# A second buffer for RWKV's chunk decay, and the decayed operands made ahead of the substitution

## The chip, the cores and the metric

The kernel runs on one core of a Trainium2 chip. The metric is the device time of one launch in microseconds; the lower, the better. The engines are named TensorE (PE, with its weight loads as PEld), VectorE (DVE), ScalarE (ACT), GpSimd (POOL) and SyncE (SP), which here issues most DMA transfers.

## What is computed

A decoder trunk of two layers on 512 tokens of width 1024, in f32. Each layer has a SwiGLU half step, a mixer of three head groups (forgetting attention "FoX", RWKV-7 time mixing, block-sparse attention "MoBA"), cross attention to 256 memory tokens, and a second SwiGLU half step. The change touches the RWKV part alone. What matters of the reference:

```python
def step(state, inp):
    r_t, w_t, k_t, v_t, kk_t, a_t = inp
    sa = jnp.einsum('bhij,bhj->bhi', state, -kk_t)
    state = (state * w_t[:, :, None, :] + sa[..., None] * (kk_t * a_t)[:, :, None, :]
             + v_t[..., None] * k_t[:, :, None, :])
    return state, jnp.einsum('bhij,bhj->bhi', state, r_t)
...
_, ys = lax.scan(step, state0, xs)
y = ys.transpose(1, 0, 2, 3)
mean = jnp.mean(y, axis=-1, keepdims=True)
var = jnp.mean(jnp.square(y - mean), axis=-1, keepdims=True)
y = ((y - mean) * lax.rsqrt(var + RWKV_GN_EPS)).reshape(B, S, W) * ln_w + ln_b
```

There are eight RWKV heads of 64. The recurrence over 512 tokens is done in eight chunks of 64 tokens.

## The kernel before

TensorE multiplies each f32 projection as three products of split operands (`three`, lines 153 to 155; the same in `ztok`, lines 952 to 954), and so most of the time goes to projections whose weights stream from HBM through a ring of three buffers.

In the mixer, RWKV heads go in four pairs (hp = 0 to 3), one head on each half of the 128 partitions. Each pair passes six stages, and `ORDER` (lines 37 and 38) names them in the order in which they are written: s (`rwkv_scaled`), g (`rwkv_gram`), r (`rwkv_rows`), i (`rwkv_inverse`), t (`rwkv_transitions`), y (`rwkv_states`), mixed with projections (R, K, V, p, fq, fk, fv, mq, mk, mv) and with attention blocks (f01, f10, ...). A scheduler turns this into one fixed order of instructions for each engine: it takes what is ready by priority (`PRI` gives leads to stages), against a timeline of its own, and a tile whose buffer is still being read holds back the instruction that would write it. On the chip each engine then works through its own queue in order. So a new buffer or an edit in one stage can move instructions of other stages.

The names in the stages:
- `Dt` (line 663) is the decay from the chunk's start to each token, and `DC` (line 668) is its last column, the decay over the whole chunk, copied out by VectorE (line 669). `DC` has one buffer; `Dt` has one too.
- `ER` holds the decayed kk and r, `B` holds b and u divided by the decay (lines 683 and 702). The Gram stage multiplies `B` with `ER` (line 722) and evicts masked products into `G` and `BN` (line 726).
- The substitution (lines 741 to 745) inverts 16x16 blocks of `G` by 30 small instructions on GpSimd. Its input `A` goes from `G` through DRAM (`scA`) by DMA, its results `Pf` and `Tf` return through DRAM as well. The inverse stage reads them (line 814 first).
- In the rows stage line 789 multiplies `B` in place with `DC` on GpSimd (`ENG["B2"]` is "g"), TensorE transposes the product (line 793), ScalarE evicts it into `BN`.
- The states stage is a serial chain over the chunks: a matmul of `AR` with the state (line 907), then two VectorE updates (line 911) that multiply the old state with `DC`. After it come a group norm (lines 920 to 925) and transposes (line 932).

Helper lines: 283 is every `tt` (so the substitution, B2 and others show as L283), 278 and 276 are copies on VectorE and ScalarE, 1023 scales a softmax row, 1026 transposes it.

## Time and profile before

| | us |
|---|---|
| runs, median of 3 | 2562.94 (2560.49 to 2565.93) |
| profiled execution, its own time | 2553.76 |
| its span, first to last instruction | 2552.1 |
| TensorE busy | 2470.5 (97%) |
| VectorE busy | 1339.3 (52%) |
| ScalarE busy | 860.2 (34%) |
| GpSimd busy | 490.0 (19%) |

A share of busy time is a mean over stages with different limits. The mixer of layer 0 lies between about 400 and 760 us of the span, that of layer 1 between about 1660 and 2020. Where TensorE waits there is read from the waits, and what else ran at that moment from the instructions in order of time; the granted clock of TensorE is given for each stretch as a share of full speed.

### The profile page before, as it was taken

The numbers are of one execution on the slowest core, as the hardware profiler recorded it, in microseconds if no ns is written. First come the engines' busy times: TensorE is split into PE (matmuls) and PEld (weight loads), VectorE is DVE, ScalarE is ACT, GpSimd is POOL, SyncE is SP. The second block draws the span as 40 slices with busy tenths as digits, with TensorE's granted clock in tenths as the row PEclk, the third lists the DMA queues.
The fourth block names the chain that finished last, engine by engine and source line by source line (L and its number), as shares of the span: only waits on it lengthen the run. The fifth ranks groups of instructions, "written<-read, shape, count | busy, mean of one in ns | idle before, by whom it ended". The sixth has DMA issues, their size and how long they took to land.

```text
span 2552.1 us, 35229 instructions
## 1 busy us (share of the span) xinstructions
PE 2470.5 (97%) x13976; PEld 2019.5 (79%) x13976; DVE 1339.3 (52%) x2503; ACT 860.2 (34%) x1401; POOL 490.0 (19%) x612
## 2 busy tenths in 40 slices
PE   8999999899889899999999999999999898999999
PEld 7888887688767788888888888877877677888887
DVE  6444345666765564343444444465776666544443
ACT  4222233233353352232332222332334543422221
POOL 4212030222210122020221111202322110311211
PEclk9999999899989999999999999999989999999999
DMA  4333343221212133333333333422211220333332
GB/s 151 99 91 96 102 121 91 52 74 36 68 55 79 50 94 99 93 97 99 91 100 99 97 98 93 129 76 67 63 46 49 69 85 28 114 99 100 99 94 80
DMA packets 434881, 218.42 MB, mean 86 GB/s; under 512 B 63856, under 2 KB 428828, under 8 KB 434716
## 3 DMA queue, kind: packets, MB, share of 16 engines
q1 hardware_dynamic: 431948, 212.36, 29.3%
q10 hardware_dynamic: 2448, 2.76, 0.3%
q8 instruction: 110, 1.80, 0.3%
q0 software_dynamic: 320, 1.05, 0.1%
q14 instruction: 55, 0.45, 0.1%
HBM read 205.64 MB, written 10.49 MB: 85 GB/s over the span
## 4 chain that ended last, share of the span: by engine, by line
PE 88%; DVE 4%; POOL 3%; DMA 2%; ACT 1%; issue 1%; SPq 1%; POOLq 0%; DVEq 0%; ACTq 0%
PE acc L153 23%; PE acc L154 23%; PE acc L155 23%; PE acc L952 1%; PE po L1055 1%; PE acc L954 1%; PE acc L953 1%; PE sp L1043 1%; PE sp L153 1%; PE sp L154 1%; PE sp L155 1%; POOL P L283 1%; PE ty L722 1%; POOL T L283 1%; PE ts L862 1%
## 5 line engine op out<-in xcount | busy, mean ns | idle before, releaser
L146 ACT ACTIVATE whi<-wraw 128x1024 fp32r<-128x1024 f32 (+3 forms) x386 | 389.7, 1012 | 1147.2 <-PE acc L154 1040.6
L153 PE MATMUL acc<-xh,whi 128*128 128x512 f32 x1776 | 697.2, 394 | 7.3 <-DVE p L500 5.1
L155 PE MATMUL acc<-xh,wlo 128*128 128x512 f32 x1776 | 695.5, 392 | 0.0
L154 PE MATMUL acc<-xl,whi 128*128 128x512 f32 x1776 | 695.4, 392 | 0.0
L147 DVE TENSOR_TENSOR wlo<-wraw,whi 128x1024 fp32r<-128x1024 f32 (+3 forms) x386 | 533.7, 1384 | 128.2 <-ACT whi L146 125.7
L153 PEld LDWEIGHTS acc<-xh,whi 128*128 128x128 f32 x1776 | 334.9, 189 | 83.7 <-DVE p L500 7.4
L155 PEld LDWEIGHTS acc<-xh,wlo 128*128 128x128 f32 x1776 | 335.0, 189 | 72.1 <-DVE wlo L147 1.0
L154 PEld LDWEIGHTS acc<-xl,whi 128*128 128x128 f32 x1776 | 335.3, 189 | 69.8
L343 POOL TENSOR_TENSOR up<-up,g 128x512 f32<-128x512 f32 x88 | 123.1, 1399 | 994.8 <-ACT whi L146 868.0
L154 PE MATMUL acc<-tl,whi 128*128 128x512 f32 x704 | 273.9, 389 | 0.0
L153 PE MATMUL acc<-th,whi 128*128 128x512 f32 x704 | 273.5, 389 | 0.0
L155 PE MATMUL acc<-th,wlo 128*128 128x512 f32 x704 | 273.4, 389 | 0.0
L342 DVE TENSOR_TENSOR up<-acc,rsb 128x512 f32<-128x512 f32 x88 | 60.8, 691 | 276.0 <-PE acc L155 276.0
L296 DVE SCALAR_TENSOR_TENSOR x<-acc,x 128x512 f32<-128x512 f32 x96 | 65.9, 690 | 265.6 <-PE acc L155 265.6
L339 DVE TENSOR_TENSOR g<-acc,rsb 128x512 f32<-128x512 f32 x88 | 60.8, 691 | 199.5 <-PE acc L155 196.5
L154 PEld LDWEIGHTS acc<-tl,whi 128*128 128x128 f32 x704 | 132.2, 188 | 27.4
L153 PEld LDWEIGHTS acc<-th,whi 128*128 128x128 f32 x704 | 132.2, 188 | 27.4
L155 PEld LDWEIGHTS acc<-th,wlo 128*128 128x128 f32 x704 | 132.2, 188 | 27.3
L241 POOL TENSOR_TENSOR sqacc<-sqacc,sq 128x512 f32<-128x512 f32 x48 | 77.1, 1607 | 360.8 <-ACT sq L240 360.5
L347 POOL TENSOR_TENSOR tl<-up,th 128x512 fp32r<-128x512 f32 x88 | 128.1, 1456 | 63.9 <-ACT th L346 63.9
L346 ACT ACTIVATE th<-up 128x512 fp32r<-128x512 f32 x88 | 55.7, 633 | 124.9 <-POOL up L343 124.9
L952 PE MATMUL acc<-whi,xh 128*128 128x256 f32 x256 | 77.2, 302 | 0.3 <-DVE p L500 0.3
(354 smaller groups left out, 3091.2 us busy)
## 6 DMA issues: line engine op xcount, KB each, us to landing
wraw<-in_ffn_w_in_dram SPq DMA_DIRECT2D x176, 512.0 KB
wraw<-in_ffn_w_out_dram SPq DMA_DIRECT2D x64, 512.0 KB
wraw<-in_mix_w_in_dram SPq DMA_DIRECT2D x52, 512.0 KB
wraw<-in_ffn_w_out_dram SPq DMA_DIRECT2D x32, 384.0 KB
wraw<-in_xattn_w_kv_dram SPq DMA_DIRECT2D x16, 512.0 KB
wraw<-in_mix_w_out_dram SPq DMA_DIRECT2D x16, 384.0 KB
scx<-x SPq DMA_DIRECT2D x16, 256.0 KB
x<-scx SPq DMA_DIRECT2D x16, 256.0 KB
```

What stands on the lines that cost most here:

```text
L146: nc.scalar.activation(hv, v, AF.Copy)
L147: nc.vector.tensor_sub(lv, v, f32(hv))
L153: mm(ps, lh, rh, start=start, stop=False)
L154: mm(ps, lh, rl, start=False, stop=False)
L155: mm(ps, ll, rh, start=False, stop=stop)
L241: (nc.vector if m == KC - 1 else nc.gpsimd).tensor_tensor(self.sqacc, self.sqacc, sq, op=ALU.add)
L296: self.nc.vector.scalar_tensor_tensor(xm, ps, coef, xm, op0=ALU.mult, op1=ALU.add)
L339: nc.vector.tensor_tensor(g, pss[0], rsb, op=ALU.mult)
L342: nc.vector.tensor_tensor(up, pss[1], rsb, op=ALU.mult)
L343: nc.gpsimd.tensor_tensor(up, up, g, op=ALU.mult)
L347: nc.gpsimd.tensor_tensor(tl, up, f32(th), op=ALU.subtract)
L952: mm(o, a, wh[:, kk, :], start=k == 0, stop=False)
```

## The change

`DC` gets two buffers, and the product of `B` with `DC` (line 789) moves from the rows stage to the Gram stage, behind the masked evictions and ahead of the DMA transfers and the substitution. Engine and shape stay.

```diff
-RW = {"e": 2, "tk1": 2, "tk2": 2, "zr": 2, "zv": 2, "ER": 2, "zk": 2, "BN": 2}
+RW = {"e": 2, "tk1": 2, "tk2": 2, "zr": 2, "zv": 2, "ER": 2, "zk": 2, "BN": 2, "DC": 2}
...
                     nc.vector.tensor_tensor(dst, pg[h][:, :, i], self.gmask[:, i:i + 1, :].to_broadcast([P, 4, 64]), op=ALU.mult)
             yield
 
+        B2 = B.rearrange("p q (i a) b -> p (q i) (a b)", i=2)
+        self.tt("B2", B2, B2, st["DC"].to_broadcast([P, 8, P]), ALU.mult)
+
         scA, scP, scT = (x[hp % 2] for x in (self.scA, self.scP, self.scT))
...
         self.cp("x", KX[:, :, 1, :], px)
         yield
-
         B2 = B.rearrange("p q (i a) b -> p (q i) (a b)", i=2)
-        self.tt("B2", B2, B2, st["DC"].to_broadcast([P, 8, P]), ALU.mult)
         for q in range(2):
```

What this does to the order is shown at three places. Line numbers of the change are up to three higher than before behind line 728.

GpSimd, layer 1, third head pair, before: `T` and `P` are the substitution's two tiles, and `B<-B,DC` is the moved product.

```order
L283 TENSOR_TENSOR T_14815<-A_14809,P_14814 64x2x14
L283 TENSOR_TENSOR P_14814<-P_14814,T_14815 64x2x14
L283 TENSOR_TENSOR B<-B,DC 128x1024
L664 MEMSET Dt 128x8
L283 TENSOR_TENSOR T_14815<-A_14809,P_14814 64x15
L283 TENSOR_TENSOR P_14814<-P_14814,T_14815 64x15
L747 COPY I_14848<-P_14814 64x256
```

GpSimd, the same place in the change:

```order
L283 TENSOR_TENSOR B<-a,Di 128x4x128
L664 MEMSET Dt 128x8
L283 TENSOR_TENSOR pT<-p 128x1024
L901 MEMSET tk_15095 128x512
L283 TENSOR_TENSOR B<-B,DC 128x1024
L283 TENSOR_TENSOR u<-zk,u 128x512
L283 TENSOR_TENSOR T_14816<-A_14810,P_14815 64x15
L283 TENSOR_TENSOR P_14815<-P_14815,T_14816 64x15
```

The product moved from inside the substitution to ahead of its first instruction. It stood inside in the last pair of both layers too; in the second pair of both layers and the third of layer 0 it stood behind the substitution; in the first pair of both it stood ahead already. In the change it stands ahead in all eight. In layer 0's third pair `pT<-p` (the squares of the MoBA keys) and `u<-zk,u`, which stood ahead of the substitution, now stand inside it.

VectorE, layer 0, second head pair, before: the start of its state updates (`tk_4945`, L911), among the softmax instructions of attention.

```order
L278 COPY mk<-sp 128x512
L911 SCALAR_TENSOR_TENSOR tk_4945<-tk_4945,DC,ts 64x64 x2
L1020 TENSOR_REDUCE mx<-sp 128x1 x2
L911 SCALAR_TENSOR_TENSOR tk_4945<-tk_4945,DC,ts 64x64 x2
L1022 RECIPROCAL sm<-sm 128x1
L1023 TENSOR_SCALAR p<-p,sm 128x256
```

VectorE, the same updates in the change (L912), from behind the second of them. Lines 994 and 1001 are the norm and gain of the MoBA keys, and their RoPE (L1006 to L1009) follows.

```order
L270 SCALAR_TENSOR_TENSOR hr<-rt,ry 128x16
L994 TENSOR_TENSOR p<-p,hr 128x1024
L684 SCALAR_TENSOR_TENSOR zr<-zr,params_80,u 128x512
L912 SCALAR_TENSOR_TENSOR tk_4945<-tk_4945,DC,ts 64x64 x2
L1001 TENSOR_TENSOR p<-p,gm 128x1024
```

The updates moved from among attention's instructions to among the keys' norm and RoPE. The copies of `DC` moved as well: the second pair's stood behind the first pair's last update, and now stands in the pair's own scaling stage, ahead of all of them.

TensorE, end of layer 1's mixer, before: the last state matmul of the last head pair (L907), its gate (L928, L929), and the transposes of the normed states (L932). `mhl` is the memory, whose key projection the triples of L153 to L155 are.

```order
L154 MATMUL acc<-mhl,whi 128x256
L155 MATMUL acc<-mhl,wlo 128x256
L907 MATMUL ts<-tk_16200,AR 128x128
L928 MATMUL ts<-gs_13077,g_16197 128x512
L929 MATMUL ts<-gs_13116,g_16197 128x512
L932 MATMUL ts<-ident,tk_16241 128x128 x4
L1026 MATMUL pt<-ident,p 128x128 x4
```

TensorE, the same place in the change, from the gate on (now L929, L930):

```order
L929 MATMUL ts<-gs_13077,g_16197 128x512
L930 MATMUL ts<-gs_13116,g_16197 128x512
L153 MATMUL acc<-mhl,whi 128x256
L154 MATMUL acc<-mhl,whi 128x256
L155 MATMUL acc<-mhl,wlo 128x256
```

With these three, 21 matmuls of that projection stand between the gate and the transposes (now L933), where none stood; the state chain of the last pair moved ahead of them. In layer 0 this place reads as before.

## Rows read from the trace of the kernel before

**Rows 1.** The page: busy time, share of the span and instructions of each engine; and the chain of work that ended last, by engine.

```profile
PE 2470.5 (97%) x13976; PEld 2019.5 (79%) x13976; DVE 1339.3 (52%) x2503; ACT 860.2 (34%) x1401; POOL 490.0 (19%) x612
...
PE 88%; DVE 4%; POOL 3%; DMA 2%; ACT 1%; issue 1%; SPq 1%; POOLq 0%; DVEq 0%; ACTq 0%
```

**Rows 2.** Busy time in stretches of 10 us of the two mixer stages: the stretch, its length, then busy us (and instructions) of PE, PEld, DVE, ACT and POOL, the granted clock, the share of the DMA engines and GB/s. The first three are of layer 0, the others of layer 1.

```profile
610.00:620.00 10.00, 9.36 (x66) 7.31 (x66) 6.89 (x24) 2.82 (x11) 7.61 (x27) 1.00 0.02 3
...
690.00:700.00 10.00, 6.32 (x33) 4.27 (x32) 5.35 (x12) 3.56 (x8) 4.55 (x13) 0.84 0.14 14
700.00:710.00 10.00, 9.14 (x138) 6.85 (x136) 3.83 (x10) 3.42 (x9) 0.00 (x0) 0.82 0.24 54
...
1820.00:1830.00 10.00, 8.65 (x78) 6.52 (x78) 9.06 (x31) 4.73 (x10) 2.55 (x6) 1.00 0.53 115
...
1870.00:1880.00 10.00, 7.24 (x52) 5.50 (x51) 7.88 (x22) 5.14 (x15) 7.16 (x20) 1.00 0.00 0
1880.00:1890.00 10.00, 10.00 (x58) 6.18 (x57) 4.22 (x14) 2.60 (x6) 1.24 (x4) 0.56 0.34 60
```

**Rows 3.** What TensorE waited for: the waiting engine, tile and line, the releaser, then us in total, times, the longest. The first two rows are of layer 0 (480 to 760 us), the last two of layer 1 (1800 to 2020 us).

```profile
PE pt L1026 <- DVE p L1023: 3.3, 2, 2.7
...
PE ty L793 <- POOL B L283: 0.9, 2, 0.5
...
PE pt L1026 <- DVE p L1023: 2.3, 1, 2.3
...
PE ty L793 <- POOL zt L523: 1.4, 1, 1.4
```

**Rows 4.** Layer 1, third head pair, all engines in order of time: start us, us, engine, line, operation, tiles, and the idle time before it with its releaser.

```profile
1875.56 0.29 DVE L1023 TENSOR_SCALAR p<-p,sm 128x128 f32<-128x128 f32 x1
...
1877.01 0.17 DVE L669 COPY DC<-Dt 128x8 f32<-128x8 f32 x1
...
1877.29 2.06 DVE L1023 TENSOR_SCALAR p<-p,sm 128x128 f32<-128x128 f32 x1
1877.33 1.89 POOL L283 TENSOR_TENSOR B<-B,DC 128x1024 f32<-128x1024 f32 x1 [1.56 <-DVE sm L1022]
...
1879.50 0.30 PE L1026 MATMUL pt<-ident,p 128*128 128x128 f32 x1 [2.29 <-DVE p L1023]
```

**Rows 5.** Layer 0, fourth head pair, the same view.

```profile
686.51 1.89 POOL L283 TENSOR_TENSOR B<-B,DC 128x1024 f32<-128x1024 f32 x1
...
686.75 1.68 DVE L269 SCALAR_TENSOR_TENSOR rt<-rt,ry 128x8 f32<-128x8 f32 x1
...
687.81 0.23 PE L1049 MATMUL sp<-maskb,identb 128*128 128x128 bf16 x1
...
689.38 1.02 PE L1043 MATMUL sp<-fox,qz 128*128 128x512 f32 x2
```

**Rows 6.** Groups of GpSimd's instructions, each shape apart: count, busy us, mean ns of one, and the idle time before them in all with what ended it.

```profile
L283 POOL TENSOR_TENSOR B<-B,DC 128x1024 f32<-128x1024 f32 x8 | 15.2, 1903 | 7.1 <-PE ty L722 4.5 <-DVE sm L1022 1.6 <-PE sp L1049 1.0
...
L283 POOL TENSOR_TENSOR u<-zk,u 128x512 f32<-128x512 f32 x8 | 10.3, 1291 | 43.7 <-DVE u L674 22.6 <-DVE rt L269 15.5 <-DVE ry L270 5.6
...
L283 POOL TENSOR_TENSOR pT<-p 128x1024 f32<-128x1024 f32 x4 | 9.0, 2256 | 46.5 <-ACT p L971 46.5
```

**Rows 7.** Layer 0 in order of time: the first pair's Gram evictions on VectorE with the product beside them and the mask product behind; and the first instruction of the second pair's substitution.

```profile
481.13 0.43 DVE L726 TENSOR_TENSOR G<-ty,gmask 128x256 f32<-128x256 f32 x1 [1.91 <-PE ty L722]
481.28 1.90 POOL L283 TENSOR_TENSOR B<-B,DC 128x1024 f32<-128x1024 f32 x1 [2.85 <-PE ty L722]
481.47 0.41 DVE L726 TENSOR_TENSOR BN<-ty,gmask 128x256 f32<-128x256 f32 x1
...
482.54 1.89 DVE L283 TENSOR_TENSOR tk<-G,lmask 64x512 f32<-64x512 f32 x2
...
549.38 0.22 POOL L283 TENSOR_TENSOR T<-A,P 64x15 f32<-64x15 f32 x1 [14.68 <-DMA A<-scA]
```

**Rows 8.** End of layer 1's mixer, TensorE in order of time: two matmuls of the memory's projection, one behind the other, the second half of the gate, and the transposes of the normed states.

```profile
1992.55 0.28 PE L155 MATMUL acc<-mhl,wlo 128*128 128x256 f32 x1
1992.67 0.28 PE L153 MATMUL acc<-mhl,whi 128*128 128x256 f32 x1
...
2000.98 1.12 PE L929 MATMUL ts<-gs,g 32*128 32x512 f32 x2
2006.08 1.08 PE L932 MATMUL ts<-ident,tk 128*128 128x128 f32 x4 [3.98 <-DVE tk L925]
```

**Rows 9.** Layer 0's mixer: groups of VectorE's instructions (count, busy us, mean ns of one), and one state step of the second head pair on TensorE in order of time.

```profile
L911 DVE SCALAR_TENSOR_TENSOR tk<-tk,DC,ts 64x64 f32<-64x64 f32 x48 | 13.3, 277 | 4.4 <-PE ts L907 3.4
...
L283 DVE TENSOR_TENSOR tk<-G,lmask 64x512 f32<-64x512 f32 x8 | 6.0, 748 | 0.1
...
L684 DVE SCALAR_TENSOR_TENSOR zr<-zr,params,u 128x512 f32<-128x512 f32 x4 | 3.0, 746 | 1.6 <-POOL u L283 1.5
...
L993 DVE TENSOR_TENSOR p<-p,hr 128x1024 f32<-128x1024 f32 x2 | 2.4, 1224 | 0.0
L1000 DVE TENSOR_TENSOR p<-p,gm 128x1024 f32<-128x1024 f32 x2 | 2.4, 1224 | 0.0
...
617.07 0.49 PE L907 MATMUL ts<-tk,AR 128*128 128x128 f32 x2
617.39 0.56 PE L905 MATMUL ts<-KV,BN 128*128 128x64 f32 x4
```

## Prediction

> **What bounds the kernel.** I read the page first: TensorE is busy for 2470.5 of 2552.1 us, and the chain that ended last is TensorE for 88% [rows 1]. So the kernel is bound by TensorE, and a change that adds or removes no matmul can act only on the 82 us in which TensorE stands idle and on the clock that it is granted. Next I read the busy time by stretches in the two layers' mixer stages, where the edited code runs [rows 2]: look there for stretches with little TensorE time, and for the stretch behind them in which the granted clock is below 1.00. Then I read what TensorE waited for [rows 3], and at the two worst places the instructions of all engines in order of time [rows 4, 5].
>
> In those rows the moved product, which I call B2 (B times DC, line 789, on GpSimd), appears as a releaser and as something worse. TensorE's transposes of B2 (L793) waited 0.9 us in layer 0 and 1.4 us in layer 1 [rows 3]; that last wait is booked to a tiny memset that stands right behind B2 on GpSimd. In layer 1, third head pair, B2 started at 1877.33, as soon as DC had been copied (1877.01 to 1877.18); it took 1.89 us, and for that whole time a VectorE multiply of 128x128 that had taken 0.29 us a moment earlier took 2.06. TensorE's transpose of that multiply's result waited 2.29 us [rows 4]. In the 10 us around this place TensorE was busy for 7.24 only, and in the next 10 us the granted clock was 0.56, that is near the lower of its two levels (1.2 of 2.4 GHz), while TensorE was busy throughout [rows 2]. In layer 0, fourth head pair, B2 at 686.51 held a 128x8 instruction of VectorE for 1.68 us, and TensorE, done at 688.04, got its next matmul at about 689.3 [rows 5].
>
> **The change part by part.** No instruction is added or removed: eight B2 of 1.90 us [rows 6], eight DC copies, the same transposes.
>
> *Second DC buffer.* With one buffer the copy of a head pair's DC stands on VectorE behind the state updates (L911) of the pair before it, and all that reads or overwrites what the copy reads (the next pair's Dt, then its ER product) stands behind the copy. With two buffers the copy of the second pair moves up into its own scaling stage. In the order of the change the pair after it gets its ER product ahead of, not behind, the previous pair's state updates. The buffer costs 8 floats a partition and no time.
>
> *B2 ahead of the substitution.* In six of the eight head pairs B2 moves on GpSimd from behind or inside the substitution to ahead of it; the first pair of each layer had it there already. Ahead of the substitution GpSimd waits for the round trip of G through DRAM anyway: 14.68 us in the second pair of layer 0 [rows 7]. So six times 1.90 us of GpSimd lie in a wait of that kind and cost nothing; if that cover were gone, the substitution would start 1.9 us later each time. Where B2 stood inside the substitution (the last pair of layer 0, the last two of layer 1) the inverse can start 1.9 us earlier, and another 1.6 us where B2 itself waited [rows 4].
>
> *What TensorE gets back.* The direct waits: 0.9 + 1.4 [rows 3] + 2.3 [rows 4] + 1.2 [rows 5] = 5.8 us. Bounds 2.3 (only the waits on the transposes) and 8.5 (with the 2.7 us that the next softmax step of layer 0 waited [rows 3]). I take 5.8, since each has its B2 beside it.
>
> *The clock.* 10 us at 0.56 cost 4.4 us of full speed [rows 2]. Where TensorE was idle for only 1.35 of 10 us (1820 to 1830) the clock stayed at 1.00. Without the 2.29 us wait the stretch before the drop would stand at about 0.5 idle. Bounds: 0 (it drops anyway) and 7.0 (layer 0 too: 6.32 us busy at 0.84 and 9.14 at 0.82 over 690 to 710 cost 1.0 + 1.6). I take 4.4, layer 1 alone, because in layer 0 the 2.7 us softmax wait stays.
>
> *End of layer 1's mixer.* There TensorE waited 3.98 us for the group norm of the last pair's states (L932) [rows 8]. In the order of the change the last pair's chain stands earlier, and 21 projection matmuls that stood ahead of the chain's end stand inside that wait. At 0.12 us each [rows 8] they fill 2.5 us of it. Bounds 0 (if the chain itself slips back) and 2.5. I take 2.5. In layer 0 the order there is unchanged.
>
> *What it costs in layer 0.* The order of the change puts the second pair's state updates between RoPE's instructions on VectorE, where attention stood before. Between the third and seventh of them VectorE has two 128x1024 products (2 x 1.22), L684 (0.75), four small products (estimate 0.9, from the 1.22 by width) and five pairs of updates (5 x 0.55): 6.9 us [rows 9]. TensorE has five steps of about 0.85 us (0.88 from the start of one to its end [rows 9]) and, by the order, some 1.0 us of other matmuls in that time, 5.25 in all, so it idles about 1.6 us; the stretch in which the chain lay before had 0.64 us of idle [rows 2], so 1.0 more. Since each step also hands over twice between the engines I take 1.5; bounds 0 and 6 (1.5 and a clock drop like the 4.4 of layer 1). Also, the third pair's substitution now has in its middle a square of 2.26 us and a product of 1.29 [rows 6] that stood ahead of it: its result lands up to 3.5 us later. Bounds 0 and 3.5; I take 1.0, since attention stands between.
>
> *VectorE beside B2.* In the first pair, where B2 stands in the Gram stage already, the evictions of G next to it take their usual 0.41 to 0.43 us, and the two mask products behind them took 1.89 [rows 7] where two take 1.5 by the mean [rows 9]: 0.4 us of VectorE that only the inverse, many us later, needs. So I count the moved collisions at nothing. The Trainium skill, page "SBUF — State Buffer", section "SBUF: two separate sides", says that GpSimd and VectorE share a port pair as an exclusive lock for a whole instruction, so that the loser blocks; it speaks against any move of B2 next to VectorE work with two SBUF inputs. The rows of 1.68, 1.89 and 2.06 us agree with it. By it all six moved B2 would cost VectorE at least those 0.4 us each, and if all of that were on the path the sum would be 2.4 us smaller.
>
> Sum: 5.8 + 4.4 + 2.5 - 1.5 - 1.0 = 10.2 us. The rows are of one execution of 2553.8 us (span 2552.1, so 1.7 us lie around it), for which the sum gives 2543.6. The median of the runs is 2562.9, 9.1 above that execution, so I take the 10 us off the median: **2553 us**.
>
> **The rivals.** *The gaps form again elsewhere.* The order of 300 us per layer is laid anew. In layer 0 the third pair's seven state steps (0.88 us each, 6 us in all [rows 9]) leave the attention stretch before 700 and now stand among projections, where TensorE had no gap. Attention then has less to fill its softmax waits, such as the 2.7 us one [rows 3]. Speaking for it: TensorE's work is the same, and the softmax chains that it waits for are no shorter. Against it: the waits that B2 makes are gone in any case. If the 5.8 us come back as new waits, and half of the 4.4 us of clock with them, 2.2 us are left: 2561, no change. *A queue stall, slower.* In layer 0's third pair GpSimd's in-order queue now has the square of the MoBA keys inside the substitution. It waits for ScalarE's copy of the projection; the four such squares waited 46.5 us in all, 11.6 each [rows 6]. If the keys come late, the substitution stands still behind it, its result lands 11 us late, and TensorE, whose inverse stands right behind, waits and loses clock (4.4): 2562.9 - 10.2 + 11.6 + 4.4 = 2569. It decides from a stall of some 10 us; against it speaks that the keys' projection stands ahead of the stretch in TensorE's order. *The change does nothing:* excluded, the order shows B2 moved in six of eight places.
>
> **How the numbers follow.** Forecast 0.50, gaps again 0.31, queue stall 0.19. Of the second I give 0.02 to the faster side, of the third 0.02 to no change. A difference within 0.2% (5.1 us) is no change here. Faster 0.52, same 0.31, slower 0.17. The forecast's own range goes from 2545 (8.5 + 7.0 + 2.5 and no cost) to 2557 (5.8 and the 2.5, without the clock, at the costs taken, would give 2557). The range for all is 2544 to 2568.
>
> **What would show it.** In the profile after, B2 stands ahead of the substitution's first instruction in all eight pairs; TensorE no longer waits for GpSimd at the transposes; no VectorE instruction of a softmax or a group norm takes 1.5 us or more beside B2; the granted clock of layer 1's third pair stays at 1.00; the wait for the last group norm of layer 1 is about 1.5 us where it was 3.98. I am wrong if TensorE's idle time in the mixer stages is not smaller, if the clock drops in layer 0's second pair of states, or if GpSimd stands still inside a substitution.

## The result and the profile after

| | before | change |
|---|---|---|
| median of 10 runs, us | 2557.64 (2540.47 to 2567.18) | 2582.25 (2569.5 to 2591.46) |
| ratio, 95% interval | | 1.0097 [1.0073, 1.0121] |
| profiled execution, its span, us | 2553.76, 2552.1 | 2587.9, 2586.2 |

The change is some 25 us slower, where 10 us less was forecast; the time lies above the range. (The median before, 2562.94 us of three runs in the prediction, is 2557.64 of ten.) The page after, busy time by engine and the engines of the chain that ended last (compare [rows 1]):

```profile
PE 2495.2 (96%) x13976; PEld 2036.8 (79%) x13976; DVE 1340.7 (52%) x2503; ACT 860.5 (33%) x1401; POOL 495.8 (19%) x612
...
PE 86%; DVE 5%; POOL 3%; DMA 3%; issue 2%; ACT 1%; SPq 1%; POOLq 0%; DVEq 0%; ACTq 0%
```

The same 13976 matmuls are busy 24.7 us longer, and the rest of the span grew by 9.4 us (91.0 after, 81.6 before). So of 34.1 us most is matmuls that ran slower, not TensorE standing still. The stretches of the mixers after, in the columns of [rows 2], show where (the last four are of layer 1):

```profile
600.00:610.00 10.00, 9.88 (x82) 7.91 (x79) 5.76 (x11) 5.66 (x11) 4.73 (x9) 1.00 0.45 113
610.00:620.00 10.00, 5.29 (x28) 4.21 (x28) 9.52 (x24) 0.00 (x0) 8.67 (x20) 0.75 0.00 0
620.00:630.00 10.00, 9.61 (x67) 8.30 (x66) 5.60 (x15) 4.00 (x9) 2.61 (x8) 0.57 0.31 52
...
710.00:720.00 10.00, 5.59 (x55) 4.31 (x56) 2.14 (x6) 2.35 (x7) 0.00 (x0) 0.70 0.30 60
720.00:730.00 10.00, 10.00 (x120) 7.29 (x117) 2.38 (x6) 1.82 (x5) 0.00 (x0) 0.50 0.01 2
730.00:740.00 10.00, 10.00 (x68) 6.82 (x66) 3.95 (x9) 2.85 (x9) 0.52 (x1) 0.61 0.01 2
...
1980.00:1990.00 10.00, 7.53 (x55) 4.52 (x57) 5.16 (x18) 2.40 (x6) 0.00 (x0) 0.86 0.41 77
1990.00:2000.00 10.00, 10.00 (x121) 7.32 (x118) 3.70 (x9) 3.60 (x8) 0.53 (x1) 0.50 0.01 2
...
2030.00:2040.00 10.00, 6.77 (x44) 5.05 (x42) 5.85 (x25) 3.39 (x5) 0.00 (x0) 1.00 0.16 52
2040.00:2050.00 10.00, 7.27 (x47) 6.17 (x48) 5.40 (x13) 7.06 (x20) 7.50 (x6) 0.66 0.57 184
```

Each time a stretch with little TensorE time is followed by one with a granted clock of 0.50 to 0.66: 0.50 is the lower of the two levels, what lies between is a mean of both. In the first three of these TensorE is busy for 9.6 to 10 of the 10 us, in the last for 7.27. What TensorE waited for, layer 0 (400 to 800 us) and then layer 1 (1660 to 2060):

```profile
PE pt L1027 <- DVE p L1024: 4.9, 4, 1.9
PE ts L908 <- DVE tk L912: 4.6, 4, 3.3
PE ty L815 <- DMA Tf<-scT: 4.0, 4, 3.2
...
PE ts L933 <- DVE tk L926: 3.4, 1, 3.4
PE ty L815 <- DMA Tf<-scT: 2.9, 2, 2.5
```

The same waits before (lines one lower, and the same two windows):

```profile
PE ty L814 <- DMA Tf<-scT: 2.8, 3, 1.7
PE ts L907 <- DVE tk L911: 1.8, 4, 0.9
...
PE ty L814 <- DMA Tf<-scT: 0.5, 1, 0.5
```

TensorE's waits for B2 [rows 3] are gone. Two waits that were there before have grown: those of the state steps (L908, the matmul behind the updates L912; the longest in layer 0 went from 0.9 to 3.3 us) and those of the inverse's first matmul (L815), which waits for `Tf` to return through DRAM (the longest from 1.7 to 3.2 us in layer 0 and from 0.5 to 2.5 in layer 1). I call the two places in layer 0 A and B. A, the second pair's states, all engines in order of time:

```profile
604.80 0.34 POOL L283 TENSOR_TENSOR T<-A,P 64x15 f32<-64x15 f32 x1 [7.24 <-DMA A<-scA]
...
607.28 1.89 POOL L283 TENSOR_TENSOR pT<-p 128x1024 f32<-128x1024 f32 x1
609.13 0.26 POOL L283 TENSOR_TENSOR P<-P,T 64x39 f32<-64x39 f32 x1
609.20 1.22 DVE L991 TENSOR_REDUCE hr<-pT 128x16 f32<-128x1024 f32 x1 [2.88 <-POOL pT L283]
...
614.53 1.38 DVE L269 SCALAR_TENSOR_TENSOR rt<-rt,ry 128x16 f32<-128x16 f32 x1
614.63 1.25 POOL L283 TENSOR_TENSOR u<-zk,u 128x512 f32<-128x512 f32 x1
...
616.58 0.80 PE L908 MATMUL ts<-tk,AR 128*128 128x128 f32 x2 [3.30 <-DVE tk L912]
```

VectorE's keys' norm (L991) waits for the squares, which stand inside GpSimd's substitution; behind it on VectorE stand the state updates, and TensorE waits for those. VectorE itself was busy for 9.52 of the 10 us from 610 on. L269 takes 1.38 us beside `u`, where its neighbours of that shape took 0.17 and 0.28. The Trainium skill, page "SBUF — State Buffer", section "SBUF: two separate sides", calls the port pair of the two engines a lock for a whole instruction, which the engine that starts first holds; this row agrees as to its end, 0.03 us behind that of `u`, though by the profile L269 had started 0.10 us ahead of `u`. B, the fourth pair:

```profile
682.60 1.90 POOL L283 TENSOR_TENSOR B<-B,DC 128x1024 f32<-128x1024 f32 x1 [8.48 <-PE ty L722]
...
695.57 0.22 POOL L283 TENSOR_TENSOR T<-A,P 64x15 f32<-64x15 f32 x1 [11.07 <-DMA A<-scA]
...
714.82 0.47 PE L815 MATMUL ty<-Tf,tk 64*64 64x64 f32 x2 [3.22 <-DMA Tf<-scT]
```

B2 was made 13 us ahead of the substitution and on GpSimd hid under its wait, as forecast. On VectorE it was not free:

```profile
682.66 2.05 DVE L1024 TENSOR_SCALAR p<-p,sm 128x384 f32<-128x384 f32 x1
684.64 0.41 DVE L726 TENSOR_TENSOR G<-ty,gmask 128x256 f32<-128x256 f32 x1
684.86 0.52 PE L1027 MATMUL pt<-ident,p 128*128 128x128 f32 x3 [1.02 <-DVE p L1024]
```

A softmax multiply beside B2 took 2.05 us (in layer 1's last pair 1.83, where the one ahead of B2 took 0.40). TensorE waited 1.02 us for it, and the evictions of `G`, which begin the round trip that ends with `Tf`, stood behind it.

To compare runs I cut each mixer at the first Gram matmul and at the sum of the next norm, and added up, in stretches of 5 us, idle time (length less TensorE busy) and clock loss (busy times one minus the granted clock). Length less both was 343 to 348 us in every mixer whose split is given here but those with added matmuls. "Fox gates" is the stage from L561 to layer 1's first Gram matmul, "A" and "B" are idle + clock loss in layer 0 from 120 to 190 and from 205 to 270 us behind the first Gram matmul.

| us | layer 0 (idle, clock) | A | B | fox gates, layer 1 | layer 1 (idle, clock) |
|---|---|---|---|---|---|
| before | 375.8 (21.4, 9.7) | 3.1+0.0 | 6.8+3.2 | 40.3 | 377.4 (19.5, 10.8) |
| change | 396.8 (28.4, 24.7) | 5.5+5.6 | 9.7+12.5 | 47.0 | 384.2 (21.4, 18.6) |

Layer 0's mixer is 21.0 us longer, layer 1's 6.8. The 6.7 us of the fox gates are not the change's: their order is the same in all kernels, and the stage took 39 to 43 or 45 to 47 us in kernels of every kind, before in both ways (47.0 in layer 0, 40.3 in layer 1). Two such stages can account for scatter of several us between runs, and for the profiled pair differing by 34 us where the medians differ by 25. The mixers scatter less: e1 and e2 below have the orders of the change and of before, and their four mixers (395.4 and 384.4, 375.0 and 378.1 us) lie within 1.4 us of these.

In layer 1 the change gains at one place and loses at the other. In the stretch that is called A in layer 0 its idle time and clock loss went from 4.6+6.6 to 3.9+3.3 us, 4.0 less, since the collision of [rows 4] and the drop behind it are gone; in that of B they went from 2.4+0.0 to 4.1+7.8, 9.5 more, behind the wait of 2.5 us for `Tf`.

### The profile page after: what moved, and what is told of

The parts are those of the page before. It is cut to its first block, busy times and chain, and to the rows that moved or that the text cites. A ratio compares the mean times of both kernels' runs of the same rounds, so it can differ in the third digit from the quotient of the medians.

```text
span 2586.2 us, 35235 instructions
## 1 busy us (share of the span) xinstructions
PE 2495.2 (96%) x13976; PEld 2036.8 (79%) x13976; DVE 1340.7 (52%) x2503; ACT 860.5 (33%) x1401; POOL 495.8 (19%) x612
## 4 chain that ended last, share of the span: by engine, by line
PE 86%; DVE 5%; POOL 3%; DMA 3%; issue 2%; ACT 1%; SPq 1%; POOLq 0%; DVEq 0%; ACTq 0%
PE acc L153 23%; PE acc L154 22%; PE acc L155 22%; PE po L1056 1%; PE sp L1044 1%; POOL T L283 1%; POOL P L283 1%; PE acc L953 1%; PE sp L153 1%; PE sp L154 1%; PE sp L155 1%; PE acc L954 1%; PE acc L955 1%; PE pt L1027 1%; PE ts L863 1%
## 5 line engine op out<-in xcount | busy, mean ns | idle before, releaser
L153 PE MATMUL acc<-xh,whi 128*128 128x512 f32 x1776 | 700.0, 395 | 5.8 <-DVE p L500 4.3
L155 PE MATMUL acc<-xh,wlo 128*128 128x512 f32 x1776 | 698.0, 393 | 0.0
L153 PEld LDWEIGHTS acc<-xh,whi 128*128 128x128 f32 x1776 | 336.4, 189 | 83.6 <-DVE p L500 5.6
L155 PEld LDWEIGHTS acc<-xh,wlo 128*128 128x128 f32 x1776 | 336.1, 189 | 72.5 <-DVE wlo L147 1.0
L153 PE MATMUL acc<-th,whi 128*128 128x512 f32 x704 | 273.6, 390 | 0.0
L155 PE MATMUL acc<-th,wlo 128*128 128x512 f32 x704 | 273.5, 389 | 0.0
L153 PEld LDWEIGHTS acc<-th,whi 128*128 128x128 f32 x704 | 132.2, 188 | 27.5
L155 PEld LDWEIGHTS acc<-th,wlo 128*128 128x128 f32 x704 | 132.1, 188 | 27.4
```

What stands on the lines that cost most here:

```text
L153: mm(ps, lh, rh, start=start, stop=False)
L155: mm(ps, ll, rh, start=False, stop=stop)
```

## The experiments

The experiments are numbered e1 to e18, with the number at each result. A result begins with the ratio of the medians to the kernel before, run beside it, and its 95% interval, then the median in us; what follows is of one profiled execution: the length of each layer's mixer, and A and B as idle time + clock loss. Diffs are cut to what matters. Lines that a table of waits names differ by up to nine between kernels, where text was added; the tile names are the same.

**Which half.**

```diff
-RW = {"e": 2, ..., "BN": 2}
+RW = {"e": 2, ..., "BN": 2, "DC": 2}
```

> Two buffers for DC, B2 left in the text of rwkv_rows. The order on all five engines is then, row for row, that of the changed kernel, so the line that moves B2 does nothing by itself. Theory A (the order laid anew makes the loss): ratio to the kernel before 1.007 to 1.012, as the changed kernel. Rival B (the place of B2 in the text, with what it does to GpSimd, makes the loss): the same order cannot differ, so B has to be false as far as the text goes; a ratio near 1.000 would mean that something other than the order counts (addresses, code).

Measured, e1: 1.009 [1.0064, 1.0117], 2577.17 us; layer 0 395.4 us, layer 1 384.4. The order of all engines is that of the change, row for row.

```diff
         self.tt("B2", B2, B2, st["DC"].to_broadcast([P, 8, P]), ALU.mult)   # in rwkv_gram, one buffer
```

> B2 written in rwkv_gram, DC left with one buffer. The order on all five engines is that of the kernel before, row for row. Theory A: ratio 1.000, within 0.003, and it shows how far two kernels of one order lie apart. Rival B: over 1.005.

Measured, e2: 0.9991 [0.9963, 1.0018], 2553.13 us; the order is that of before. So the moved text does nothing: the scheduler places B2 by when `DC` can be written. The buffer is the whole change, order and time.

**B2 early without the rest of the new order.**

```diff
+        Dt = st["Dt"] = rw.tile([P, 8, 65], F32, name="Dt", tag="Dt")
...
+        self.tt("B2", B2, B2, st["Dt"][:, :, 64:65].to_broadcast([P, 8, P]), ALU.mult)
```

> DC keeps one buffer; B2 reads its factors from Dt itself, so it no longer waits for the copy of DC and goes ahead of the substitution in all pairs, while the order of layer 0 on TensorE stays as before but for a few matmuls (the second pair's states and the attention stay interleaved). This is the part of the change that the prediction's 5.8 us of waits rest on. Theory A (early B2 is harmless or a gain, the rest of the new order is the loss): 2 to 12 us faster than before, ratio 0.995 to 0.999, and no TensorE wait over 3 us in layer 0 for Tf or for the state update. Rival B (an early B2 costs, by contention with VectorE or by what it displaces on GpSimd): 5 us or more slower, ratio 1.002 to 1.010.

Measured, e3: 1.0055 [1.0034, 1.0077], 2571.65 us; layer 0 382.7, layer 1 384.8 us. The waits for B2 are gone and layer 1's third pair keeps the clock at 1.00, yet it is slower: rival B's range, though not by its cause. A is 1.9+0.0 and B 6.6+10.8 us. The stretches of the fourth pair in layer 0, and the one wait in them:

```profile
690.00:700.00 10.00, 6.30 (x32) 3.46 (x33) 2.60 (x6) 1.89 (x5) 0.92 (x2) 0.76 0.37 66
700.00:710.00 10.00, 10.00 (x128) 8.54 (x128) 3.12 (x9) 2.14 (x5) 0.00 (x0) 0.50 0.01 2
710.00:720.00 10.00, 10.00 (x85) 6.20 (x85) 4.41 (x10) 2.55 (x7) 0.00 (x0) 0.67 0.01 2
```

```profile
697.22 0.47 PE L814 MATMUL ty<-Tf,tk 64*64 64x64 f32 x2 [3.70 <-DMA Tf<-scT]
```

In [rows 2] the same stretch, 690 to 700, was busy for 6.32 us at 0.84: the idle time is equal, in all of B too (6.8 and 6.6 us), but there it came in pieces (2.74 the longest) and the clock stood at 0.82 behind it, here in one of 3.70 and at 0.50. Counted from the first Gram matmul, `Tf` came 3.0 us earlier than before (227.7 against 230.7), and TensorE was done with the matmuls ahead of it 5.8 us earlier (224.0 against 229.8), since the small waits ahead were gone.

```diff
+        DB = st["DB"] = rw.tile([P, 8, 1], F32, name="DCB", tag="DCB")
+        nc.vector.tensor_copy(DB, DC)     # DC has two buffers, DCB one; B2 and the states read DCB
```

> DC has two buffers and is copied early, so Dt comes free early; B2 and the states read a second copy of it (8 added VectorE copies of 128x8, some 0.06 us each) which has one buffer, so B2 stays behind or inside the substitution. Theory A: the scaling stage moves but the second pair's states stay beside the attention, so near the kernel before, ratio 0.998 to 1.004, with the waits for B2 (about 1 to 2 us each) still there. Rival C (the early release of Dt and ER is by itself what spoils the order): ratio 1.006 to 1.012, as the changed kernel.

Measured, e4: 1.0033 [1.0011, 1.0054], 2564.21 us; layer 0 387.6, layer 1 380.4; A 3.5+1.3, B 7.3+7.9. That is in theory A's range, but layer 0's mixer is 11.8 us longer than before with B2 behind or inside the substitution in three of its four pairs: the early copy of `DC` costs without the early B2.

**Filling the wait for Tf.** The added matmuls write a bank that the next ones overwrite.

```diff
+            with self.tc.issue_after(self.score[-2].ins):
+                for _ in range(4):
+                    last = mm(p1..., self.ident[0:64, :], st["G"][0:64, 0:8]..., start=True, stop=True)
```

> The kernel with B2 early alone (B2 reads Dt, one DC buffer), whose fourth head pair showed one TensorE wait for Tf of 3.7 us in layer 0 and 5.3 us in layer 1, each followed by some 25 us at a granted clock of 0.50 to 0.68. Here TensorE gets four added matmuls of 128x512 in that wait (about 1.1 us each, 4.4 in all, into the bank that the next matmuls overwrite; work that the result doesn't need); the order of all its other matmuls stays, row for row. Theory A (the loss is the clock that falls behind the wait; the wait itself is no longer than what was saved ahead of it): the clock stays at 1.00 behind both places, some 10 us come back per layer, so 15 to 22 us faster than the kernel with B2 early alone, and 2 to 10 us faster than the kernel before, ratio 0.996 to 0.999. Rival D (the chain through DRAM is what costs, the clock is only a symptom): the time stays, ratio 1.004 to 1.008, with the clock high.

Measured, e5: 0.9982 [0.9956, 1.0007], 2551.64 us; layer 0 374.7 (17.4, 6.8), layer 1 376.4 us. To hold the order, the edit also changes the places and leads of some stages (so do e6, e7 and e10); some 27 of TensorE's 13976 other entries still moved. The same stretches:

```profile
690.00:700.00 10.00, 9.38 (x56) 5.15 (x58) 4.11 (x8) 1.88 (x5) 1.30 (x4) 1.00 0.37 66
700.00:710.00 10.00, 9.71 (x163) 6.64 (x159) 4.28 (x13) 3.79 (x10) 0.00 (x0) 1.00 0.01 2
710.00:720.00 10.00, 10.00 (x143) 8.14 (x140) 4.95 (x14) 5.34 (x14) 0.52 (x1) 1.00 0.02 3
```

`Tf` comes no sooner (228.3 us behind the first Gram matmul, 227.7 in e3), and 0.7% (8 us in each mixer) comes back from matmuls whose results nobody reads: what e3 lost was clock. Theory A held; against the kernel before the gain is not clear of the noise.

```diff
+        after = self.tc.issue_after(self.score[-1].ins) if hp == 3 else contextlib.nullcontext()
```

> The kernel with B2 early alone, with one thing moved in the whole order: the scores of the next softmax's second head (about 1.2 us of TensorE) stand ahead of the first matmul that needs Tf instead of behind it. Theory A: the wait for Tf shrinks from 3.7 to about 2.5 us in layer 0 and from 5.3 to about 4 in layer 1, the clock still falls behind at least the longer one: 2 to 10 us back, ratio 1.001 to 1.005. Rival D: no difference beyond the moved work, ratio 1.004 to 1.008.

Measured, e6: 1.003 [1.0002, 1.0059], 2564.72 us; waits for Tf of 2.9 and 4.3 us, mixers 382.8 and 383.1 us. The ratio is in theory A's range, but layer 0's mixer is as long as in e3 and the intervals of the two overlap: one score of useful work ahead is not enough.

```diff
+                for _ in range(3):        # the same in the changed kernel
+                    last = mm(p1..., self.ident[0:64, :], st["G"][0:64, 0:8]..., start=True, stop=True)
```

> The changed kernel with three added matmuls of 128x512 (3.3 us; work that the result doesn't need) in the wait of 3.2 us for Tf in layer 0's fourth head pair. In layer 0 the order of all else stays as in the changed kernel; in layer 1 the scheduler lays it anew, so only layer 0 is compared. Theory A: the clock of 0.55 over 720 to 740 goes to 1.00, layer 0's mixer (396.8 us from the first Gram matmul to the next stage's norm, 375.8 before) gets 8 to 12 us back, to about 386; the other half of its loss, in the second pair's states, stays. Rival D: layer 0's mixer stays within 2 us of 396.8.

Measured, e7: 1.0062 [1.0031, 1.0093], 2570.31 us; layer 0 385.9 us, B 6.0+2.6, A 5.5+7.5. So theory A held, and B's wait is worth 11 us of layer 0's 21; the rest lies at A. (The profiled execution took 2553.5 us, 17 less than the median; both its fox gates took 40.3 us, which is outside the mixers.)

**Place A.**

```diff
-"hsq": "g"
+"hsq": "v"
```

> The changed kernel with the squares of the head norms on VectorE instead of GpSimd, so that no square stands inside a substitution and VectorE's reduce behind it never waits for GpSimd; the scheduler lays the order anew around them. Theory E (the other half of layer 0's loss is a queue stall: the square on GpSimd holds VectorE's reduce, the state updates behind it wait, TensorE gets a wait of 3.3 us): TensorE waits under 1.5 us in the second pair's states, the clock there stays at 1.00, and layer 0's mixer is 6 to 10 us shorter than 396.8. Rival F (the states' chain is simply without filler where the new order puts it): the waits of 2 to 3 us and the clock drop in the second pair's states stay.

Measured, e8: 1.0045 [1.002, 1.007], 2569.93 us; layer 0 388.5; A 7.1+6.2. No state step waits over 1.1 us, but `zr` now does, 4.0 us (it needs `u`, inside the substitution). The time is that of theory E, its cause is not: A has not shrunk, and the gain is B's (8.8+1.2).

```diff
-"hsq": "g", "ku": "g"
+"hsq": "v", "ku": "v"
```

> The changed kernel with the squares of the head norms and the product u of the scaling stage both on VectorE. With the squares alone moved, VectorE still waited 3.4 us for u, which stood inside the substitution on GpSimd, and TensorE 4.0 us behind it. Theory E (the stall in the second pair's states is GpSimd's in-order queue: whatever stands inside a substitution is late, and VectorE and TensorE wait in turn): with both moved no TensorE wait of over 1.5 us is left between the third pair's substitution's start and its end in layer 0, the clock there stays at 1.00, and layer 0's mixer goes from 396.8 (388.5 with the squares alone) to 380 to 386, the wait for Tf in the fourth pair being left. Rival F (the states' chain has no filler there): waits of over 2 us on the state updates remain and layer 0's mixer stays at 386 to 392.

Measured, e9: 1.0064 [1.0041, 1.0088], 2574.8 us; A 4.2+4.8 with no wait over 1.6 us, but the wait for Tf grew to 4.5 us and layer 0 is 397.6. Theory E missed, and rival F too.

```diff
+            with self.tc.issue_after(self.lastT.ins) if hp == 1 and c == 1 else contextlib.nullcontext():
```

> The changed kernel with one edge added to TensorE's order: the second pair's state steps from the second chunk on are issued behind the last transposes of the MoBA keys, so that they stand among the attention matmuls again, as in the kernel before; the scheduler lays the rest anew around them. Theory A (the chain of state steps had no filler where the change put it, and that is the 11 us lost in layer 0's second pair: 5.5 idle, 5.6 by the clock, against 3.1 and 0.0 before): idle time and clock loss between 120 and 190 us behind the first Gram matmul go to 2 to 4 us in all, the wait of 3.3 us for the state update is gone, layer 0's mixer is 6 to 10 us shorter than 396.8 if the wait for Tf in the fourth pair stays as it is. Rival G (the loss there comes from what GpSimd does inside the third pair's substitution, wherever the states stand): a loss of 7 us or more stays in that stretch.

Measured, e12: 1.0094 [1.0062, 1.0125], 2579.9 us; A 9.9+1.9, the wait for `zr` 6.7 us. Theory A missed; the loss is in rival G's range.

```diff
+        with self.tc.issue_after(self.sub_end.ins) if hp else contextlib.nullcontext():
             self.tt("ku", u, k, u, ALU.mult)
```

> The changed kernel with two things undone in the order: the second pair's state steps stand among the attention again (as in the run before this one, in which TensorE then waited 6.7 us for the product zr, which waits for u on GpSimd), and on GpSimd the product u of a pair stands behind the substitution of the pair before it instead of inside it. Rival G made sharper (the early release of Dt lets the next pair's scaling in, its product u gets into the substitution on GpSimd, and VectorE and TensorE wait for it): idle time plus clock loss between 120 and 190 us behind the first Gram matmul of layer 0 falls from 11.8 (11.1 in the changed kernel) to 2 to 5 us, with no wait over 2 us. Theory A for this stretch (states without filler alone): was not borne out by moving the states, so a loss of 8 us or more here would leave both theories without support.

Measured, e13: 1.0093 [1.0067, 1.0119], 2574.29 us; A 8.9+4.4, now the keys' transposes wait 7.3 us for RoPE. That leaves both theories without support.

```diff
-"hsq": "g", "ku": "g"                    # on top of e12
+"hsq": "v", "ku": "v"
```

> The changed kernel with the state steps among the attention again and both products (squares, u) on VectorE. With both on VectorE but the states left without filler the stretch lost 9.0 us (4.2 idle, 4.8 clock) in waits of 1.6 us and less. If both causes hold, states without filler and products inside the substitution, the stretch loses 2 to 5 us here; if the states' place doesn't matter, 8 to 10 us.

Measured, e14: 1.0099 [1.0075, 1.0122], 2577.31 us; A 5.1+7.1, waits of 2.6 (keys) and 2.1 (`zr`). That is more than either forecast.

```diff
+        late = self.tc.issue_after(self.ropeEnd.ins) if hp == 3 else contextlib.nullcontext()
```

> The changed kernel with the fourth pair's scaling put back in one respect: its VectorE instructions (from the decay's scaling to the product with yr) are issued behind the last RoPE instruction of the MoBA keys. In the changed kernel VectorE is busy for 9.5 of the 10 us in which TensorE idles most (610.5 to 620.5, TensorE 5.3), with three chains in its queue: this scaling, the keys' norm and RoPE, the second pair's state updates. Theory H (VectorE is the bound there, because the early release of Dt lets the scaling in beside the other two): without the scaling the stretch from 120 to 190 us behind the first Gram matmul loses 3 to 6 us instead of 11.1. Rival (two chains are enough to starve TensorE): 8 us or more. The fourth pair comes later by this, so the time as a whole may stay or grow; it is no test.

Measured, e15: 1.0149 [1.0103, 1.0196], 2594.08 us; A 5.3+6.2, the states still wait (2.2 the longest). By itself the fourth pair's scaling on VectorE is not the cause.

```diff
+        late = self.tc.issue_after(self.ropeEnd.ins) if hp == 3 else contextlib.nullcontext()
...
+            with self.tc.issue_after(self.lastT.ins) if hp == 1 and c == 1 else contextlib.nullcontext():
```

> As the run before, and the second pair's state steps among the attention again, which is the order of the kernel before in that stretch but for B2. Theory H: 2 to 4 us lost between 120 and 190 us behind the first Gram matmul of layer 0 (3.1 in the kernel before). If 8 us or more stay, VectorE's queue is not what starves TensorE there and the cause stays open.

Measured, e16: 1.009 [1.0059, 1.0121], 2572.88 us; A 5.7+6.0, the keys' transposes wait 4.9. Theory H missed.

In seven kernels (e8, e9, e12 to e16) the wait changed its releaser and A stayed at 9 to 13 us. What these had in common was the keys' projection: its last copy ended 120.0 us behind the first Gram matmul before, 119.8 in e3 and 125.0 in e4 (A 1.9 and 4.8 in all), but 132.7 in the change and 131 to 135 in the seven. The last two runs move it back.

```diff
-PRI = {..., "g1": 2500}
+PRI = {..., "g1": 2500, "mk": 9000}      # 6000 in e18
```

> The changed kernel, in which the projection, norm and RoPE of the MoBA keys (mk) have a lead of 9000 in the scheduler's priorities, where they had -1500. With the second buffer the keys' last projection copy ended 132 us behind the first Gram matmul of layer 0 (119 before), and TensorE stood behind the chain square, norm, RoPE that follows it. By the order of this kernel that copy ends at 121 to 124 us again, while the buffer, the early product B2 and the order of all that is ahead stay. Theory (the late keys cost stretch A, 120 to 190 us behind the first Gram matmul): idle plus clock loss there falls from 11.1 us to 3 to 6, no wait of TensorE for the keys or for zr above 2.5 us; the wait for Tf in the fourth pair stays, so layer 0's mixer takes 388 to 392 us (396.8 with the change), the whole 0.5% over before. Rival (the loss in A is that of VectorE or GpSimd, which have the same instructions there): A stays at 9 or more, the mixer at 395 to 399.

> The same with a lead of 6000: the keys' last projection matmul stands some 500 columns later than with 9000, and their transposes 1500 later. Theory: as with 9000 within 2 us, A 4 to 7 us, layer 0's mixer 388 to 394. Rival: 395 to 399.

Measured, e17: 0.9993 [0.9961, 1.0025], 2558.59 us: the change's loss is gone, with the buffer and the early B2 still in. The copy ended at 122.0; layer 0 took 385.7 (21.3, 18.3), layer 1 377.7. e18: 1.0042 [1.0012, 1.0072], 2566.05 us; the copy ended at 129.6 only; layer 0 388.6, layer 1 383.8. So an order with the keys earlier has none of the loss, but not by the mechanism that was expected (the new leads move other instructions too, so the keys' place alone is not shown to decide): A is 8.9 in e17 (6.3+2.6) and 8.6 in e18, near the rival's 9, where 3 to 6 had been forecast, and the larger part of e17's gain is B (3.2+10.2, where the change had 9.7+12.5; the longest wait for Tf is 0.7). Both theories missed, and a wait for `zr` above 2.5 us is there as well. In A of e17 TensorE goes through the keys and the states without a long wait, and then:

```profile
609.87 0.55 DVE L674 TENSOR_SCALAR u<-a,params,dpar 128x512 f32<-128x512 f32 x1
...
614.89 1.25 POOL L283 TENSOR_TENSOR u<-zk,u 128x512 f32<-128x512 f32 x1
616.18 0.75 DVE L684 SCALAR_TENSOR_TENSOR zr<-zr,params,u 128x512 f32<-128x512 f32 x1 [4.56 <-POOL u L283]
...
616.99 2.08 PE L686 MATMUL tx<-zr,blk 128*128 128x512 f32 x2 [4.06 <-DVE zr L684]
```

VectorE has its `u` ready at 610.42, GpSimd takes it up inside the third pair's substitution at 614.89, and VectorE and TensorE stand still for it.

**Useless matmuls elsewhere.** The last pair's output transposes wait for the group norm in both layers of the kernel before (4.0 us each, [rows 8]), and for 1.1 to 4.0 us in most of the others.

```diff
+        for _ in range(4 if hp == 3 else 0):
+            mm(pyt, g2[:, 0, :], self.gs[0], start=True, stop=True)
```

> The kernel before with the same four added matmuls ahead of the last pair's output transposes in both layers (work that the result doesn't need), nothing else. Theory A: 6 to 12 us faster than before, ratio 0.995 to 0.998. Rival D: ratio 0.999 to 1.002, since the softmaxes behind that wait are limited by the other engines.

Measured, e11: **0.9964 [0.9946, 0.9983], 2544.79 us**, faster than both kernels; theory A held. The kernel before, and then this one, from layer 1's wait on (this execution is 11.4 us ahead at that place, so its stretches are 10 us earlier):

```profile
2000.00:2010.00 10.00, 4.04 (x12) 2.08 (x12) 6.66 (x27) 5.00 (x10) 1.42 (x2) 0.70 0.29 96
2010.00:2020.00 10.00, 9.60 (x63) 7.14 (x64) 7.02 (x22) 6.95 (x26) 6.08 (x5) 0.79 0.66 211
```

```profile
1990.00:2000.00 10.00, 7.09 (x36) 3.83 (x35) 6.52 (x29) 5.55 (x13) 3.34 (x3) 1.00 0.19 55
2000.00:2010.00 10.00, 8.55 (x58) 5.12 (x58) 8.50 (x27) 6.18 (x26) 4.17 (x4) 1.00 0.67 210
```

The clock stays at 1.00 there. But between the two profiled executions the mixers differ by only 1.4 us (layer 0) and 2.2 us (layer 1), and 4.4 of the 11.4 us are the fox gates', so the traces show less of the gain than the medians (9 us) do.

The edits of e5 and e11 together:

```diff
+                for _ in range(4):        # e5, in the wait for Tf
...
+        for _ in range(4 if hp == 3 else 0):
+            mm(pyt, g2[:, 0, :], self.gs[0], start=True, stop=True)
```

> The kernel with B2 early alone and the four added matmuls in the wait for Tf (ratio 0.998), and four more matmuls of 128x512 (4.4 us; work that the result doesn't need) ahead of the last pair's output transposes, where TensorE waits 4.0 us for the group norm in both layers and the clock behind it is 0.66 to 0.70. Theory A (a wait costs its length once more through the clock): 6 to 12 us faster than without the second filling, ratio 0.994 to 0.996. Rival D: no change from 0.998, since the stage behind is limited by VectorE and ScalarE, not by the clock.

Measured, e10: 0.9993 [0.9969, 1.0017], 2558.23 us. Theory A missed. There is no usable trace (the profiled execution took 4909 us), so why the two gains do not add up stays open.

## Why the prediction was wrong

**The failing step** is "The buffer costs 8 floats a partition and no time", and with it the term for what the new order costs. The costs that the prediction saw (1.5 and 1.0 us) were those of two places of that order; e1 shows that the buffer brings the whole new order and all of the loss (1.009, 23.6 us), e2 that the moved text, a heading of its own in the prediction, brings nothing. In layer 0, whose mixer is 21.0 us longer, A lost 8.0 us more than before and B 12.2 us more, and for B the sum has no cost at all.

**The 5.8 us of direct waits.** The mechanism was right: no wait of TensorE for B2 is left. The sum was not: the 1.2 us of [rows 5] are no wait. TensorE took up the transposes of B2 in that time, after 0.42 us that are in the 0.9 already, so the four waits were 4.6 us.

```profile
688.45 1.09 PE L793 MATMUL ty<-ident,B 128*128 128x128 f32 x8 [0.42 <-POOL B L283]
```

That they would be kept was wrong. The sum did not ask what is late next. It is `Tf`: G to DRAM, substitution, back through DRAM. The matmuls ahead of it move up by the waits saved, `Tf` by less, and the pieces come back as one wait (e3: 3.70 us where 0.86 had been). This is the rival "the gaps form again elsewhere" (2561); its error was the price. It gave back half of the clock; in fact the new wait costs more clock than the old ones did. e5 shows it in e3's order (8 us in each mixer), e7 in the change's (11 us of layer 0).

**The clock, 4.4 us.** Right at its place: layer 1's third pair runs at 1.00 in e3, and from 1890 to 1920 in the change. But the two mixers of the change lose 43.3 us of clock, those of before 20.5.

**End of layer 1's mixer, 2.5 us.** The wait (L933) is 3.4 us where 3.98 was and 1.5 was forecast: 0.6 us. The 21 matmuls did fill 2.7 us behind the gate, but the norm came later:

```profile
2037.78 1.22 DVE L147 TENSOR_TENSOR wlo<-wraw,whi 128x1024 fp32r<-128x1024 f32 x1 [0.60 <-DMA wraw<-in_xattn_w_kv_dram]
2040.16 0.63 PE L933 MATMUL ts<-ident,tk 128*128 128x128 f32 x4 [3.38 <-DVE tk L926]
```

In the new order the split of a streamed weight stands on VectorE among the norm's small instructions. With its wait for the weight, 0.60 us, it held them up for 1.8 us.

**Layer 0's second pair, 1.5 us, and the third's substitution, 1.0.** The places were named right, and two of the three signs given for being wrong (clock drop in these states, no less idle time in the mixers) came true. The size was off: A lost 3.1 us before and 11.1 after, 8.0 more where 2.5 was taken. The third sign did not show: the squares start inside the substitution right behind its step and hold it for 1.9 us; their projection had come in time. So the rival "a queue stall, slower" (2569) has the right sign and the wrong mechanism: it is VectorE, and TensorE behind it, that waits for GpSimd, not GpSimd for the keys.

**B2's cover** held on GpSimd: the substitution waited 7.24 us at A and 11.07 us at B for its input behind it. "I count the moved collisions at nothing" did not: the sign that no softmax instruction takes 1.5 us or more beside B2 failed in the last pair of both layers (2.05 and 1.83 us), with 1.02 us of waiting on TensorE in layer 0.

**Open.** Why A loses 8 us more. e17 speaks against the keys' late projection alone, since A stayed at 8.9 us with the projection 10.7 us earlier (in e18, with 8.6 us, it is only 3 us earlier). Every variant shows another releaser out of one knot of norm, RoPE, scaling and states on VectorE and a substitution on GpSimd with `u` or the squares inside; no run took all of these out at once in the change's order. Also open is why the clock fell to 0.50 in e17's fourth pair behind waits of only 0.73, 0.40 and 0.21 us, so a single long wait is a cause that was shown (e5, e7), but not the only one. Where the clock fell in e3 and e17, TensorE went through the inverse's matmuls of 64x64 and less; no run tells whether they have a part in it, and e5 ran the same ones at 1.00.

## What to carry to other kernels

Under a scheduler a second buffer is an edit of the whole order, and a line moved in the text may be none: compare the orders of each half of a change by itself before pricing it. Where a stall is removed ahead of a round trip of fixed length, price the wait at the end of that round trip, and the clock behind it: at B 6.8 us of idle time in pieces came with 3.2 us of clock loss, and 6.6 us with one wait of 3.70 in it with 10.8 (e3). But 3.2 us in pieces of 0.73 and less came with 10.2 in e17, so read that price from a trace and don't work it out from the idle time. A wait that can't be removed can be worth filling with matmuls that nobody reads (e5, e11), but measure each filled wait by itself and together (e10).

## What was not expected of the hardware

The granted clock also falls where TensorE is not idle. The kernel before, fox gates of layer 0, TensorE busy for all of both stretches:

```profile
435.00:440.00 5.00, 5.00 (x34) 4.50 (x32) 1.83 (x2) 0.62 (x1) 0.10 (x1) 1.00 0.41 108
440.00:445.00 5.00, 5.00 (x22) 4.53 (x23) 2.47 (x14) 1.06 (x1) 0.09 (x1) 0.57 0.00 0
```

Ahead of the fall stand 20 matmuls of 128x4, in it eight of 128x2:

```profile
439.84 0.36 PE L583 MATMUL tx<-f,upper 128*128 128x4 f32 x2
...
440.38 0.39 PE L154 MATMUL acc<-xl,whi 128*128 128x512 f32 x1
...
441.34 0.63 PE L154 MATMUL acc<-xl,whi 128*128 128x512 f32 x1
...
442.20 1.70 PE L645 MATMUL tx<-blk,e 128*128 128x2 f32 x8
```

The projection matmuls between them go from 0.39 to 0.63 us each. In this execution the same stage with the same order took 47.0 us in layer 0 and 40.3 in layer 1, with 9.1 and 1.4 us lost to the clock; in the profiled execution of the change layer 1's took 47.0 us too, with 9.2 lost. So the lower level can come or stay away in one place without any edit. What brings it is not shown.
